# One part of the w_ada sums at double width beside the u projection, three parts beside the chunks and the GLU

## The chip, the cores and the metric

The kernel runs on one core of a Trainium2 chip. The metric is the device time of one launch in microseconds (us). TensorE is called PE here, VectorE DVE, ScalarE ACT, GpSimd POOL, and SyncE, which issues most transfers, SP. Each engine takes its instructions strictly in the order in which they were placed when the kernel was built.

## The reference, cut to what matters

```python
c_act = jax.nn.silu(c)
ada = c_act @ w_ada[l] + b_ada[l]                    # (1, 6*1024)
sh_m, sc_m, g_m, sh_f, sc_f, g_f = jnp.split(ada, 6, axis=-1)
h = modulate(rms_norm(x), sh_m, sc_m)                # h*(1+sc) + sh
proj = h @ w_in[l]                                   # z (1792 columns) and u (512)
y_rwkv = rwkv7_time_mix(z...)                        # a scan over 1024 tokens, 8 heads
y_s5 = s5_mix(u...)                                  # state-space scan, then GELU and a GLU
mix = jnp.concatenate([y_rwkv, y_s5], axis=-1) @ w_out[l]
x = x + g_m[:, None, :] * mix
h = modulate(rms_norm(x), sh_f, sc_f)
x = x + g_f[:, None, :] * ((silu(h @ w_gate) * (h @ w_up)) @ w_down)
return rms_norm(x) * final_gain
```

The six parts of `ada` are numbered 0 to 5 in this order: shift, scale and gate of the mixing half, then shift, scale and gate of the FFN half. Parts 0 and 1 are needed before the first projection, part 2 at the first output of the output projection, parts 3 and 4 for the FFN's input, part 5 at the FFN's output.

## The kernel before, in words

The kernel goes through these stages, with the times of the profiled execution: the start, where x is loaded, normed and transposed (to about 78 us); the u projection (tile `pu`, to 105 us); the z projection with the S5 scan and the preparation of the RWKV chunks (to about 425 us); the chunks of the first half of the tokens, which go on beside the GLU (tile `pglu`, to about 559 us); the output projection of the first half (tile `po`, to 642 us); and the FFN of the first half with the chunks of the second half beside it, and then the rest (to the end).

A part of `ada` is a product of a vector with a 1024 x 1024 block of `w_ada`. `ada_load` (L285) brings columns of the block into tiles `wada`, four transfers of 256 rows each. `ada_acc` (L295 to L300) forms eight products with a scalar per partition and adds them up in `acc`: the first by L295 on DVE, the others by L297 on DVE, or, where `eng` is not DVE, by a multiplication on ACT (L299) and an addition on POOL (L300). `ada_cols` (L306, L307) adds `acc` over the partitions by matmuls with a column of ones into a PSUM tile `pac` and writes `mod`, the table that every modulation and gate reads.

Parts 0 and 1 are summed in the start, 512 columns at a time: two accumulations to a part, with six `wada` tiles in the pool. Parts 2 and 3 go through `ada_steps` (L828), a generator of steps of 256 columns: four accumulations to a part, four `wada` tiles in the pool, which is what one step loads. The argument `mix` decides whose arithmetic a step is: by default every other step (columns 0 and 512 of a part) is on ACT and POOL, the others on DVE. The generator `adg` is woven with the chunks (`c0`) and the GLU (`glg`) at L1254, and its last steps with the second chunks and the finish. Parts 4 and 5 go through a second generator `adl`, all on DVE, which L1434 weaves with the output projection `o0`; L1435 runs what is left of it behind the output projection.

The weave sets the order in which the program is written. A scheduler then places the instructions of each engine by its own estimate of when their inputs are there, so that the order on an engine differs from the written one. The lines of the output projection that matter are: `outproj` loads the parts of y from memory (`yt`, L1295 and L1298), splits them in two (`yhl`, on ACT and POOL), loads and splits the weight (`wraw`, `wo`), multiplies (L1317), and at its end multiplies `po` by `gmb`, the broadcast of part 2 (L1325), and adds x (L1326). `bcast_gate` (L1266, L1267, tile `pgb`) forms `gmb` from `mod`. The finish of a chunk group (`pb`, `pd`, `pv`, `pg`; L949 to L1122) ends in `ld`, which is written to memory as `y_d` and read back as `yt`. The FFN begins with the transposition `ptr` (L1343) of the normed x, and with `pgate` behind it.

Of the kernel before, what the change touches and what calls it, by code (L numbers as in the profile page):

```python
# [29 lines left out]
def kernel(  # L30
# [45 lines left out]
    def pool(name, bufs=1, space=None, side=None, stack=ctx, reuse="tile"):  # L76
        kw = dict(name=name, bufs=bufs)
        if space is not None:
            kw["space"] = space
        if side is not None:  # L80
            kw["side"] = side
        if space != DRAM:
            kw["reuse_waits"] = reuse
        return stack.enter_context(tc.tile_pool(**kw))
# [89 lines left out]
    sp = pool("start", stack=sts, side="right")  # L174
    pst = pool("pstart", stack=sts, space=PSUM)
    pac = pst.tile([P, 512], F32, name="pac")
# [103 lines left out]
    def ada_load(pl, part, j0, n, bufs):  # L280
        c0 = 1024 * part + 128 * j0
        wts = []
        for kk in range(4):
            wt = pl.tile([P, 2, 128 * n], F32, tag="wada", bufs=bufs, name="wada")
            nc.sync.dma_start(wt, w_ada[0, 256 * kk:256 * kk + 256, c0:c0 + 128 * n].rearrange("(k p) n -> p k n", p=P))  # L285
            wts.append(wt)
        return wts

    def ada_acc(pl, wts, n, eng=V):

        acc = pl.tile([P, 128 * n], F32, tag="acc", bufs=2 if n > 2 else 3, name="acc")
        for k in range(8):
            wt = wts[k // 2][:, k % 2, :]
            if k == 0:
                V.tensor_scalar_mul(acc, wt, cact[:, 0:1])  # L295
            elif eng is V:
                V.scalar_tensor_tensor(out=acc, in0=wt, scalar=cact[:, k:k + 1], in1=acc, op0=ALU.mult, op1=ALU.add)  # L297
            else:
                S.mul(wt, wt, cact[:, k:k + 1])  # L299
                G.tensor_tensor(out=acc, in0=acc, in1=wt, op=ALU.add)  # L300
        return acc

    def ada_cols(acc, part, j0, n, ps):

        for j in range(n):
            PE.matmul(ps[:, j:j + 1], lhsT=acc[:, 128 * j:128 * j + 128], rhs=ones[:, 0:1], start=True, stop=True)  # L306
        V.scalar_tensor_tensor(out=mod[:, part, j0:j0 + n], in0=ps, scalar=1.0 if part in (1, 4) else 0.0,  # L307
                               in1=col("b_ada", 8 * part + j0, n), op0=ALU.add, op1=ALU.add)
# [50 lines left out]
    def mods(a0, a1, j0):  # L359
        ada_cols(a0, 0, j0, 4, pac[:, 256 + j0:260 + j0])  # L360
        ada_cols(a1, 1, j0, 4, pac[:, 264 + j0:268 + j0])
# [3 lines left out]
    def u_mm(hf, k, b):  # L365
        for n, (a_, b_) in enumerate(PASS):
            PE.matmul(pu[hf, b], lhsT=uw[b][:, a_, k, :], rhs=hT[hf, k][:, b_, :],  # L367
                      start=(k == 0 and n == 0), stop=(k == 7 and n == 2))
# [169 lines left out]
    wa = [ada_load(sp, part, 0, 4, 6) for part in range(2)]  # L538
# [5 lines left out]
    wa = [ada_load(sp, part, 4, 4, 6) for part in range(2)]  # L544
# [19 lines left out]
    for hf, b in ((0, 2), (0, 3), (1, 2)):  # L564
        for k in range(4):
            u_mm(hf, k, b)
    mods(*acs, 4)
    for hf in range(2):
        for k in range(4, 8):
            modulate(hf, k)  # L570
            for b in range(2):
                u_mm(hf, k, b)
    for hf in range(2):
        for b in range(2):
            u_out(hf, b)
# [250 lines left out]
    def ada_steps(pl, parts, ps, mix=lambda j: j % 4):  # L826

        todo = []  # L828
        def cols():
            acc, part, j = todo.pop(0)  # L830
            ada_cols(acc, part, j, 2, ps("pac2")[:, 0:2])
        for part in parts:
            for j in (0, 2, 4, 6):
                todo.append((ada_acc(pl, ada_load(pl, part, j, 2, 4), 2, V if mix(j) else None), part, j))
                if len(todo) > 2:
                    cols()
                yield
        while todo:
            cols()
            yield  # L840
# [301 lines left out]
    def weave(*gens):  # L1142

        gens = [g if isinstance(g, tuple) else (g, 1) for g in gens]
        while gens:
            for g in list(gens):
                for _ in range(g[1]):
                    if next(g[0], gens) is gens:
                        gens.remove(g)
                        break  # L1150
# [51 lines left out]
    def LIM(g, n):  # L1202
        for _ in range(n):
            if next(g, gens_end) is gens_end:
                return
            yield
# [43 lines left out]
    psx[1] = pool("psp2", stack=sps, space=PSUM)  # L1250
    gls, ads = ExitStack(), ExitStack()
    glg = s5_glu(pool("glp", stack=gls))
    adg = ada_steps(pool("adp2", stack=ads), (2, 3), ps_s)
    weave(c0, (LIM(glg, 18), 2), LIM(adg, 12))  # L1254

    def fd(nm):
# [170 lines left out]
    o0 = outproj(0, xp0, op, ("s", "p", "A", "G"), lambda: pool("gp", stack=gps, side="right"), "a")  # L1427
    weave(seq(c1, finishes(1)), LIM(o0, 4), LIM(late, 4))
    ras.close()
    das = ExitStack()  # L1430
    adl = ada_steps(pool("adp3", stack=das, side="right"), (4, 5), ps_a, lambda j: True)
    weave((LIM(late, 16), 2), o0, (LIM(adl, 2), 1))
    for _ in adl:
        pass  # L1434
    gps.close()  # L1435
    das.close()
    ops.close()
    sps.close()
    now[0] = PARTS[2]
# [54 lines left out]
```

## Time and profile before

| | |
|---|---|
| runs | 1585.34, 1589.63 (median), 1592.18 us |
| the profiled execution's own time | 1592.24 us |
| its span, first to last instruction | 1590.5 us |
| mean granted TensorE clock | 0.937 |
| busy PE, DVE, ACT, POOL | 89%, 60%, 36%, 33% |
| chain that ended last, by engine | PE 62%, DVE 15%, DMA 8%, POOL 7% |
| chain: DVE acc L297, DMA wada | 2% each |

The profiled execution is 2.6 us above the median of the runs and 1.7 us longer than its span. Busy time is counted for each engine; a busy matmul includes what it overlaps with the next, so a group's busy time divided by its count is longer than its pace. "Idle before" with an arrow names what ended an idle time. The granted clock is a share of 2.4 GHz: 1.00 is that level, 0.50 is 1.2 GHz.

### The profile page before, as it was taken

How to read it: one execution, taken by the hardware profiler on the slowest of the kernel's cores; microseconds unless marked ns; L12 is line 12 of the kernel's file. 1: busy time of each engine (PE TensorE's matmuls, PEld its weight loads, DVE VectorE, ACT ScalarE, POOL GpSimd, SP SyncE). 2: the span in 40 equal slices, each digit the busy share in tenths (PEclk: the TensorE clock that was granted, in tenths of full speed). 3: DMA queues.
4: the chain of work that ended last, by engine and by line, in shares of the span. 5: the costliest groups of instructions: out<-in, count | busy, mean ns of one | idle time of the engine just before them, and what ended most of it. 6: DMA issues, size and time to landing. Idle time of an engine off the chain costs nothing.

```text
span 1590.5 us, 22996 instructions
## 1 busy us (share of the span) xinstructions
PE 1421.5 (89%) x9071; PEld 1146.6 (72%) x9071; DVE 948.4 (60%) x1623; ACT 574.5 (36%) x913; POOL 532.4 (33%) x485
## 2 busy tenths in 40 slices
PE   3897898898778878598999999899997999999997
PEld 2775776677667646486777777677786888888885
DVE  6976228889696969854448855445736433333335
ACT  4442345444346453233225422224443222222223
POOL 4369344332154324145000003400251244454543
PEclk8898898998878879799999999899998999999999
DMA  9424754452645355354223224422731423233331
GB/s 292 133 88 138 204 192 144 124 127 75 135 131 148 109 153 187 118 115 100 62 63 117 90 87 99 98 76 66 225 103 38 151 84 107 88 106 93 100 99 54
DMA packets 262060, 187.67 MB, mean 118 GB/s; under 512 B 71606, under 2 KB 233024, under 8 KB 261952
## 3 DMA queue, kind: packets, MB, share of 16 engines
q1 hardware_dynamic: 258224, 178.00, 38.6%
q10 hardware_dynamic: 2912, 7.64, 1.4%
q8 instruction: 71, 1.16, 0.3%
q0 software_dynamic: 816, 0.57, 0.2%
q14 instruction: 37, 0.30, 0.1%
HBM read 157.11 MB, written 31.16 MB: 118 GB/s over the span
## 4 chain that ended last, share of the span: by engine, by line
PE 62%; DVE 15%; DMA 8%; POOL 7%; issue 4%; ACT 3%; SPq 1%; ACTq 0%; DVEq 0%; POOLq 0%
PE pup L270 14%; PE pgate L270 13%; PE pdn L270 13%; PE pz L270 5%; PE po L1317 3%; PE p L1062 3%; DVE acc L297 2%; DMA wada<-in_w_ada_dram 2%; POOL stmp L1006 2%; POOL XU L1008 2%; PE pu L367 2%; PE pY L762 1%; PE pA L962 1%; DMA XU<-x_d 1%; PE pglu L270 1%
## 5 line engine op out<-in xcount | busy, mean ns | idle before, releaser
L270 PE MATMUL pdn<-wd,act 128*128 128x512 f32 x1056 | 268.4, 396 | 0.7 <-DVE x L1366 0.5
L270 PE MATMUL pup<-h,hl_up 128*128 128x512 f32 x1056 | 267.0, 395 | 0.2 <-ACT hl_up L131 0.2
L270 PE MATMUL pgate<-h,hl_g 128*128 128x512 f32 x1056 | 262.8, 395 | 1.2 <-ACT hl_g L131 1.2
L270 PEld LDWEIGHTS pdn<-wd,act 128*128 128x128 f32 x1056 | 196.9, 189 | 46.4 <-issue 2.3
L270 PEld LDWEIGHTS pup<-h,hl_up 128*128 128x128 f32 x1056 | 197.8, 189 | 44.6 <-issue 2.6
L270 PEld LDWEIGHTS pgate<-h,hl_g 128*128 128x128 f32 x1056 | 196.6, 188 | 46.2 <-issue 3.6
L1366 DVE TENSOR_TENSOR x<-pdn,x 128x512 f32<-128x512 f32 x176 | 118.9, 688 | 177.7 <-PE pdn L270 177.0
L270 PE MATMUL pz<-hT,hl_z 128*128 128x256 f32 (+1 forms) x912 | 185.6, 360 | 22.1 <-POOL zm L866 6.7
L270 PEld LDWEIGHTS pz<-hT,hl_z 128*128 128x128 f32 x912 | 150.8, 205 | 52.8 <-ACT zo L872 9.7
L1401 DVE TENSOR_TENSOR rawd<-rawd,gfb 128x1024 f32<-128x1024 f32 x44 | 56.6, 1287 | 106.1 <-DMA rawd<-in_ffn_w_down_dram 83.9
L1317 PE MATMUL po<-wo,yhl 128*128 128x512 f32 x384 | 99.7, 415 | 5.3 <-ACT yhl L1302 2.4
L1317 PEld LDWEIGHTS po<-wo,yhl 128*128 128x128 f32 x384 | 75.1, 200 | 23.7 <-ACT yhl L1302 2.8
L131 ACT CAST hl_up<-raw_up 128x1024 fp32r<-128x1024 f32 x44 | 46.3, 1051 | 123.3 <-PE pup L270 112.0
L131 ACT CAST wd<-rawd 128x1024 fp32r<-128x1024 f32 x44 | 45.8, 1052 | 121.4 <-DVE rawd L1401 91.0
L297 DVE SCALAR_TENSOR_TENSOR acc<-wada,cact,acc 128x256 f32<-128x256 f32 (+1 forms) x112 | 72.1, 653 | 7.5 <-DMA wada<-in_w_ada_dram 6.4
L127 POOL TENSOR_TENSOR yhl<-yt,yhl 128x512 fp32r<-128x512 f32 x16 | 23.4, 1467 | 155.3 <-ACT yhl L1302 149.4
L1006 POOL TENSOR_TENSOR stmp<-LU,XU 128x126 f32<-128x126 f32 (+22 forms) x62 | 31.2, 503 | 127.2 <-DMA LU<-l_d 122.5
L127 POOL TENSOR_TENSOR hl_g<-raw_g,hl_g 128x1024 fp32r<-128x1024 f32 x19 | 45.6, 2397 | 78.9 <-ACT hl_g L131 51.3
L1395 ACT ACTIVATE sgt<-pgate 128x512 f32<-128x512 f32 x44 | 26.4, 600 | 123.5 <-PE pgate L270 123.3
L127 POOL TENSOR_TENSOR wd<-rawd,wd 128x1024 fp32r<-128x1024 f32 x19 | 49.7, 2615 | 57.4 <-ACT wd L131 57.4
L875 POOL TENSOR_TENSOR zo<-zo,zm 128x512 f32<-128x512 f32 x28 | 44.0, 1571 | 72.1 <-ACT zo L872 60.1
L127 POOL TENSOR_TENSOR hl_up<-raw_up,hl_up 128x1024 fp32r<-128x1024 f32 x19 | 49.8, 2620 | 49.5 <-ACT hl_up L131 49.5
(374 smaller groups left out, 2431.3 us busy)
## 6 DMA issues: line engine op xcount, KB each, us to landing
raw_g<-in_ffn_w_gate_dram SPq DMA_DIRECT2D x44, 512.0 KB, 4.0
raw_up<-in_ffn_w_up_dram SPq DMA_DIRECT2D x44, 512.0 KB, 4.0
rawd<-in_ffn_w_down_dram SPq DMA_DIRECT2D x44, 512.0 KB, 3.4
wada<-in_w_ada_dram SPq DMA_DIRECT2D x64, 256.0 KB, 3.1
raw_z<-in_w_in_dram SPq DMA_DIRECT2D x24, 512.0 KB, 5.7
wada<-in_w_ada_dram SPq DMA_DIRECT2D x16, 512.0 KB, 9.6
wraw<-in_w_out_dram SPq DMA_DIRECT2D x32, 256.0 KB, 4.6
zt_d<-zo SPq DMA_DIRECT2D x28, 256.0 KB, 3.0
```

The lines of the kernel that those rows point to most:

```text
L127: (eng or G).tensor_tensor(out=out, in0=a, in1=b, op=ALU.subtract)
L131: S.copy(dst[:, 0], src)
L270: PE.matmul(ps, lhsT=lf(a, k), rhs=rf(b, k), start=(n == 0), stop=(n == 3 * kb - 1))
L297: V.scalar_tensor_tensor(out=acc, in0=wt, scalar=cact[:, k:k + 1], in1=acc, op0=ALU.mult, op1=ALU.add)
L367: PE.matmul(pu[hf, b], lhsT=uw[b][:, a_, k, :], rhs=hT[hf, k][:, b_, :], start=(k == 0 and n == 0), stop=(k == 7 and n == 2))
L875: G.tensor_tensor(out=o, in0=o, in1=zm[:, 0:HT], op=ALU.add)
L1006: SOLVE.tensor_tensor(out=t, in0=LU[:, j, j + 1:32].unsqueeze(2).to_broadcast([P, nt, nk]), in1=X[:, j:j + 1, 0:nk].to_broadcast([P, nt, n ...
L1008: SOLVE.tensor_tensor(out=X[:, j + 1:32, 0:nk], in0=X[:, j + 1:32, 0:nk], in1=t, op=ALU.add)
L1062: PE.matmul(ps[r, h], lhsT=a, rhs=b, start=(n == 0), stop=(n == len(ops) - 1))
L1317: PE.matmul(pss[i], lhsT=yh[k][:, a, 128 * i:128 * i + 128], rhs=wo[:, b], start=(k == 4 and n == 0), stop=(k == 3 and n == 2))
L1366: V.tensor_tensor(out=t, in0=ps, in1=t, op=ALU.add)
L1401: V.tensor_tensor(out=raw, in0=raw, in1=gfb, op=ALU.mult)
```

## The change

Part 2 leaves the steps. Its four transfers for each half of its columns are issued after the first half of the modulations, from the pool of the start with its six tiles, and its two accumulations of 512 columns, all on DVE, are written behind the u projection's matmuls. The steps beside the chunks and the GLU now hold parts 3, 4 and 5: 12 steps of 256 columns instead of 8, every other one on ACT and POOL. The second generator beside the output projection is gone, with its pool.

```diff
@@ -565,11 +565,14 @@
         for k in range(4):
             u_mm(hf, k, b)
     mods(*acs, 4)
+    wa = [(part, j0, ada_load(sp, part, j0, 4, 6)) for part in (2,) for j0 in (0, 4)]
     for hf in range(2):
         for k in range(4, 8):
             modulate(hf, k)
             for b in range(2):
                 u_mm(hf, k, b)
+    for n, (part, j0, w) in enumerate(wa):
+        ada_cols(ada_acc(sp, w, 4), part, j0, 4, pac[:, 272 + 4 * n:276 + 4 * n])
     for hf in range(2):
         for b in range(2):
             u_out(hf, b)
@@ -1250,7 +1253,7 @@
     psx[1] = pool("psp2", stack=sps, space=PSUM)
     gls, ads = ExitStack(), ExitStack()
     glg = s5_glu(pool("glp", stack=gls))
-    adg = ada_steps(pool("adp2", stack=ads), (2, 3), ps_s)
+    adg = ada_steps(pool("adp2", stack=ads), (3, 4, 5), ps_s)
     weave(c0, (LIM(glg, 18), 2), LIM(adg, 12))
 
     def fd(nm):
@@ -1427,13 +1430,8 @@
     o0 = outproj(0, xp0, op, ("s", "p", "A", "G"), lambda: pool("gp", stack=gps, side="right"), "a")
     weave(seq(c1, finishes(1)), LIM(o0, 4), LIM(late, 4))
     ras.close()
-    das = ExitStack()
-    adl = ada_steps(pool("adp3", stack=das, side="right"), (4, 5), ps_a, lambda j: True)
-    weave((LIM(late, 16), 2), o0, (LIM(adl, 2), 1))
-    for _ in adl:
-        pass
+    weave((LIM(late, 16), 2), o0)
     gps.close()
-    das.close()
     ops.close()
     sps.close()
     now[0] = PARTS[2]
```

The placed order shows what this moves. On DVE, beside the u projection, the kernel before has the modulations (`xt`), the lower halves of their splits (`hT`), and then the first split of a z weight (`hl_z`):

```order
L307 SCALAR_TENSOR_TENSOR mod<-pac,cols 128x4 x2
L211 COPY cols<-pac 128x128
L588 TENSOR_SCALAR hbg<-cols 128x4
L589 TENSOR_SCALAR hga<-cols 128x4
L352 TENSOR_SCALAR xt<-xt,mod 128x4x128
L127 TENSOR_TENSOR hT_102<-xt,hT_102 128x512
L352 TENSOR_SCALAR xt<-xt,mod 128x4x128 x3
L127 TENSOR_TENSOR hT_104<-xt,hT_104 128x512
```

The changed kernel has this at the same place, beginning with the first of the two `mod`:

```order
L307 SCALAR_TENSOR_TENSOR mod<-pac,cols 128x4
L295 TENSOR_SCALAR acc<-wada,cact 128x512
L297 SCALAR_TENSOR_TENSOR acc<-wada,cact,acc 128x512
L307 SCALAR_TENSOR_TENSOR mod<-pac,cols 128x4
L295 TENSOR_SCALAR acc<-wada,cact 128x512
L297 SCALAR_TENSOR_TENSOR acc<-wada,cact,acc 128x512 x2
L352 TENSOR_SCALAR xt<-xt,mod 128x4x128
L297 SCALAR_TENSOR_TENSOR acc<-wada,cact,acc 128x512
L352 TENSOR_SCALAR xt<-xt,mod 128x4x128
L297 SCALAR_TENSOR_TENSOR acc<-wada,cact,acc 128x512
L127 TENSOR_TENSOR hT_102<-xt,hT_102 128x512
```

Eleven of the sixteen operations on 512 columns stand between the modulations, the last five behind the last `hT` and ahead of the first `hl_z`.

On PE, the kernel before ends the output projection with these rows, in which four sums of `ada` (`pac`) stand between the last `po` and the next half's `pb`, the gate's `pgb` and the FFN's transpositions:

```order
L1317 MATMUL po<-wo,yhl 128x512 x49
L306 MATMUL pac_5751<-ones,acc 128x1 x2
L1317 MATMUL po<-wo,yhl 128x512 x20
L306 MATMUL pac_5772<-ones,acc 128x1 x2
L306 MATMUL pac_5793<-ones,acc 128x1 x2
L306 MATMUL pac_5797<-ones,acc 128x1 x2
L306 MATMUL pac_5801<-ones,acc 128x1 x2
L949 MATMUL pb<-rz,blk 128x512
L1267 MATMUL pgb<-dgb,ones 128x128 x2
```

The changed kernel has there (line numbers past the first hunk are 3 higher):

```order
L1320 MATMUL po<-wo,yhl 128x512 x14
L924 MATMUL pn<-sq,blk 128x512
L1320 MATMUL po<-wo,yhl 128x512 x62
L952 MATMUL pb<-rz,blk 128x512
L1320 MATMUL po<-wo,yhl 128x512 x20
L965 MATMUL pA<-ar,bk 64x128 x32
L1270 MATMUL pgb<-dgb,ones 128x128 x2
```

No `pac` is left there, `pb` stands among the `po`, and 32 of the next half's `pA` stand ahead of the transpositions.

On SP, behind the last large solve of the chunks, the kernel before issues the transfers for the end of the chunk stage in this order (`y_d` written by the GLU, inputs of the next chunks `kz`, `rz`, `gz`, weights `wraw`):

```order
L285 DMA wada<-in_w_ada_dram 128x2x256 x8
L822 DMA y_d<-zz 128x4x256
L285 DMA wada<-in_w_ada_dram 128x2x256 x2
L790 DMA zz<-z_d 128x4x128 x2
L285 DMA wada<-in_w_ada_dram 128x2x256 x6
L882 DMA kz<-zt_d 128x2x256
L1123 DMA y_d<-ld 128x2x256
```

The changed kernel goes on with `wada` behind these:

```order
L285 DMA wada<-in_w_ada_dram 128x2x256 x9
L885 DMA kz<-zt_d 128x2x256
L1126 DMA y_d<-ld 128x2x256
L885 DMA rz<-zt_d 128x2x256
L885 DMA gz<-zt_d 128x256
L285 DMA wada<-in_w_ada_dram 128x2x256 x2
L825 DMA y_d<-zz 128x4x256
L285 DMA wada<-in_w_ada_dram 128x2x256 x2
L1126 DMA y_d<-ld 128x2x256
L285 DMA wada<-in_w_ada_dram 128x2x256 x7
L885 DMA kz<-zt_d 128x2x256
```

Twelve of the `wada` transfers, three steps' worth, stand behind the first inputs of the next chunks, and the second `kz` behind eleven of them.

## Rows read from the trace of the kernel before

**Rows 1.** Stretches: length, busy (instructions) PE, PEld, DVE, ACT, POOL; clock, DMA, GB/s

```profile
78.00:82.00 4.00, 4.00 (x10) 3.12 (x11) 3.97 (x8) 4.00 (x6) 1.75 (x2) 0.50 0.00 0
82.00:105.00 23.00, 22.89 (x100) 18.38 (x98) 13.35 (x9) 9.76 (x12) 12.51 (x5) 1.00 0.35 115
500.00:559.00 59.00, 46.68 (x637) 38.53 (x635) 53.85 (x122) 29.63 (x59) 19.47 (x20) 0.89 0.42 127
...
574.80:642.00 67.20, 58.00 (x231) 44.11 (x232) 59.18 (x94) 22.76 (x36) 30.69 (x22) 0.91 0.53 164
642.00:661.40 19.40, 6.17 (x23) 4.86 (x23) 16.08 (x45) 4.05 (x10) 0.00 (x0) 0.58 0.49 151
661.40:683.00 21.60, 16.96 (x175) 14.64 (x173) 16.55 (x24) 6.99 (x11) 8.29 (x6) 0.98 0.32 86
683.00:750.00 67.00, 62.31 (x380) 49.95 (x379) 33.14 (x48) 21.18 (x33) 32.89 (x69) 0.96 0.48 108
```

**Rows 2.** Timeline of PE, finish and output projection: start, length, row [idle before]

```profile
558.99 2.07 PE L949 MATMUL pb<-rz,blk 128*128 128x512 f32 x2 [1.00 <-DVE rz L946]
...
574.76 10.17 PE L1317 MATMUL po<-wo,yhl 128*128 128x512 f32 x32 [2.44 <-ACT yhl L1302]
588.24 2.08 PE L1121 MATMUL pg<-gs,g2w 128*128 128x256 f32 x4 [3.30 <-DVE ld L1122]
...
637.27 4.80 PE L1317 MATMUL po<-wo,yhl 128*128 128x512 f32 x20
...
648.25 1.01 PE L306 MATMUL pac<-ones,acc 128*128 128x1 f32 x4 [5.77 <-DVE mod L307]
653.96 0.98 PE L306 MATMUL pac<-ones,acc 128*128 128x1 f32 x4 [4.70 <-DVE acc L297]
657.46 0.98 PE L306 MATMUL pac<-ones,acc 128*128 128x1 f32 x4 [2.51 <-DVE tcol L246]
...
661.41 0.85 PE L1343 MATMUL ptr<-dg,x 128*128 128x128 f32 x3
```

**Rows 3.** Timeline of PE, u projection

```profile
77.94 26.95 PE L367 MATMUL pu<-hT,hl_u 128*128 128x512 f32 x108 [0.37 <-ACT hT L351]
```

**Rows 4.** Timeline of DVE, u projection

```profile
86.60 0.68 DVE L127 TENSOR_TENSOR hT<-xt,hT 128x512 fp32r<-128x512 f32 x1
96.92 1.68 DVE L127 TENSOR_TENSOR hl_z<-raw_z,hl_z 128x1024 fp32r<-128x1024 f32 x1 [9.65 <-PE pu L367]
```

**Rows 5.** Groups by line and shape, 0 to 120 us: busy, mean ns | idle before

```profile
L297 DVE SCALAR_TENSOR_TENSOR acc<-wada,cact,acc 128x512 f32<-128x512 f32 x28 | 24.5, 882 | 1.8 <-DMA wada<-in_w_ada_dram 1.5
```

**Rows 6.** Groups by line and shape, 425 to 530 us

```profile
L300 POOL TENSOR_TENSOR acc<-acc,wada 128x256 f32<-128x256 f32 x28 | 21.7, 777 | 2.2 <-ACT ar L1081 0.6 <-issue 0.3 <-ACT wada L299 0.3
L297 DVE SCALAR_TENSOR_TENSOR acc<-wada,cact,acc 128x256 f32<-128x256 f32 x28 | 16.0, 570 | 1.0 <-DMA wada<-in_w_ada_dram 0.8
```

**Rows 7.** Timeline of DVE, first and last row of five ada steps, and one step

```profile
483.23 0.35 DVE L295 TENSOR_SCALAR acc<-wada,cact 128x256 f32<-128x256 f32 x1
...
494.22 0.34 DVE L295 TENSOR_SCALAR acc<-wada,cact 128x256 f32<-128x256 f32 x1
...
527.34 0.48 DVE L297 SCALAR_TENSOR_TENSOR acc<-wada,cact,acc 128x256 f32<-128x256 f32 x1
```

**Rows 8.** Timeline of SP, chunks and GLU: the issue of eight ada loads

```profile
484.54 16.69 SPq L285 DMA_DIRECT2D wada<-in_w_ada_dram  x8
```

**Rows 9.** Timeline of DVE, one pair of operations at two places

```profile
514.81 3.31 DVE L1114 SCALAR_TENSOR_TENSOR lrs<-ld,cols,lrs 128x256 f32<-128x256 f32 x2
...
531.93 0.87 DVE L1114 SCALAR_TENSOR_TENSOR lrs<-ld,cols,lrs 128x256 f32<-128x256 f32 x2
```

**Rows 10.** Timeline of POOL beside the first of these

```profile
514.19 2.79 POOL L127 TENSOR_TENSOR zhl<-zz,zhl 128x1024 fp32r<-128x1024 f32 x1
```

**Rows 11.** Groups by line and shape, 559 to 661.4 us

```profile
L1325 DVE TENSOR_TENSOR yo<-po,gmb 128x512 f32<-128x512 f32 x8 | 5.5, 685 | 0.0
```

**Rows 12.** Timeline of PE, 740 to 750 us

```profile
746.39 1.92 PE L1028 MATMUL pG<-XU,ak 32*32 32x32 f32 x64 [4.69 <-DMA XU<-x_d]
```

## The prediction

> **What bounds the kernel now.** I read the page's engine shares and its chain first: PE is busy 89% of the span and holds 62% of the chain, so the change can only pay where PE waits. Then I read the busy times by stretch [rows 1]. From 500 to 559 us DVE is the full engine, 53.85 of 59.00 us, and PE has 12.3 us free. From 574.8 to 642 us PE has 58.00 and DVE 59.18 of 67.20 us: neither is full, so they wait for each other. From 642 to 661.4 us PE has only 6.17 of 19.40 us, at a granted clock of 0.58, against 0.91 in the stretch before. That is the hole the change aims at. The timeline of PE says what is in it [rows 2]: three sums of ada columns whose waits, 5.77, 4.70 and 2.51 us, add up to 13.0 us, all for DVE. From 683 us on PE is nearly full again (62.31 of 67.00).
>
> Everything behind 750 us has the same work on every engine, so I price five places: the u projection, the chunk stage, the finish with the output projection, the 22 us behind it, and one wait at 746 us. The sum is made against the profiled execution's own 1592.24 us, which lies 2.6 us over the median of the runs, 1589.63; what comes out is taken off that median.
>
> **1. The u projection.** Sixteen operations on 128x512 come to DVE. At 882 ns [rows 5] they are 14.1 us, taking the two first products as long as the others. In the kernel before, DVE does its last lower half at 86.60 and idles 9.65 us before 96.92 [rows 4]. Eleven new operations stand ahead of that lower half: 11 x 0.882 = 9.7, so it ends at 97.0 instead of 87.3. PE runs 108 matmuls from 77.94 to 104.89 [rows 3], 0.25 us each, and the last six need that lower half: 97.0 + 1.5 = 98.5 still lies before 104.9. The other five operations end at 101.5, the first z weight's lower half (1.68 us) at 103.2, also before. So the work lies beside PE's, and what it costs is that PE meets some lower halves late in the middle of its list, and eight small matmuls. The transfers, 4.2 MB, have room: the DMA share is 0.00 and 0.35 in these stretches [rows 1], though they now stand among the z weights' loads. The bounds: nothing, and +6 if DVE's surplus over its idle time, 14.1 - 9.65 = 4.5, is all paid, with 1.5 for a late transfer. I take +2, nearer to the lower end because the end times fit.
>
> **2. The chunks and the GLU.** Four steps are added, two on DVE, two on ACT and POOL. A DVE step is seven times 0.570 [rows 6] and a first product of 0.35 [rows 7], 4.3 us; of the other kind DVE does only the first product, and POOL 7 x 0.777 = 5.4 us [rows 6]. So DVE gets 2 x 4.3 + 2 x 0.35 = 9.3 us more, POOL 10.9. DVE has 5.2 us free from 500 to 559 [rows 1]. In the placed order the GLU's last norm, some 3 us by an estimate (four operations like L1114's and three as long), leaves this stretch and comes behind the next chunks' `bo`. DVE's list up to there is longer by 9.3 - 3 = 6.3. By the pace of the steps: the five that the kernel before has behind its solve take 527.82 - 483.23 = 44.6 us, 8.9 each [rows 7]. The changed order has nine there: 483.23 + 9 x 8.9 = 563.3, which is 4.3 behind the start of `pb` (558.99). Both readings give +4 to +7; I take +7, since DVE is full here and nothing hides it. The lower bound is 0 (the idle time and the stretch without any ada step from 528 to 559 take it all). The upper bound is the slowest gap between steps, 494.22 - 483.23 = 11.0 [rows 7]: nine of these end at 582.2, +23.
>
> **3. The finish and the output projection.** From `pb` (558.99) to the first transposition (661.41) the kernel before takes 102.4 us [rows 2]. Rebuilt without ada:
> - To the matmuls of the projection. Before, the second pair of `pg` ended at 590.32 after waiting 3.30 us for DVE [rows 2]. Now all `pg` stand before `po`: 590.32 - 558.99 - 3.3 = 28.0 us, as if no `po` went ahead.
> - The 192 `po`. The stretch of 67.20 us has 58.00 us of busy PE [rows 1], of which about 5 are the second `pg` and five sums of ada; 53 are left, and 1 for waits for PSUM banks. At 20 in 4.80 us [rows 2] the `po` alone would be 46.
> - The tail. Four tiles, each a product and an addition of 0.685 us on DVE [rows 11], are 5.5 us; with 3 for the squares and the norm, 8.5. Before, it was 661.41 - 642.07 (637.27 + 4.80) = 19.3 [rows 2], with the 13.0 us of ada waits in it.
>
> 28 + 54 + 8.5 = 90.5, so -12. Bounds: -19 if DVE without its sums of ada lets `po` begin 7 us sooner (before, 32 of them began at 574.76 [rows 2]); -4 if the remaining 160 `po` of before set the pace, (642.07 - 590.32) x 192 / 160 = 62.1 instead of 54. I take the middle, -12.
>
> **4. Behind it.** From 661.4 to 683 PE is idle 4.6 of 21.60 us while DVE has 16.55 [rows 1]. Part of the next chunks' preparation now stands ahead of the transpositions. I take about half, -2.5, between -4.6 and 0.
>
> **5. The wait at 746 us.** PE waits 4.69 us for `XU`, read back from memory [rows 12]. The changed order has 165 matmuls of the FFN before that place instead of 221. The chain that it waits for also starts earlier. Between -4.7 and +5; I take -1.5.
>
> Sum: 2 + 7 - 12 - 2.5 - 1.5 = -7. On the profiled execution 1585.2, on the median **1582.6**, forecast 1583. The forecast's own range is -13 to 0, 1576 to 1590.
>
> **The rivals.**
>
> *A, the chunk stage absorbs the steps.* For it: no step runs from 528 to 559 us, and PE has 12.3 us free there. Against it: DVE is full at 53.85 of 59. Terms 1 and 2 at 0, term 3 at -14: -18, 1572.
>
> *B, the steps set the pace (slower).* The pool has four `wada` tiles, one step's load, and SP issues in order: it spent 16.69 us on eight such transfers because each waits for a tile to come free [rows 8]. In the changed order eleven `wada` issues stand ahead of the second `kz`, and the last sum of ada ahead of `bo`. What queues behind SP's waits is `kz`, `rz`, `wraw` and `yt`, so the preparation and the output projection wait too. At 11.0 us a step term 2 is +23, and the sum 2 + 23 - 12 - 2.5 - 1.5 = +9: 1599. It turns the sign once term 2 passes +14, and counts as slower by 0.5% from +22. Against it: the later steps of before ran at less than 9 us.
>
> *C, DVE and POOL block each other.* A pair of L1114 took 3.31 us at 514.81 [rows 9], while a split of 2.79 us ran on POOL [rows 10], and 0.87 at 531.93 [rows 9]: 2.4 us lost beside one POOL operation. If each of the 14 new POOL additions held DVE up by its own length, 10.9 us, term 2 would be +18 and the sum +4: 1594. Against it: the additions of before ran beside DVE steps of 0.570 mean, not twice as long. The Trainium skill ("SBUF — State Buffer", section "Who interferes with whom") has the rule for it: DVE and GpSimd share a pair of ports as an exclusive lock, so a DVE instruction with two inputs in SBUF is shut out while a GpSimd instruction reads SBUF. The trace agrees with it at 514.81, where L1114 reads two tiles; by that rule moving steps onto POOL is not free for DVE, and its result is this rival's.
>
> *D, the output projection doesn't stream.* If `po` waits for the loads and splits of `yhl` and `wo` rather than for DVE, term 3 is -4 and the sum +1: 1591. For it: the `po` at 574.76 waited 2.44 us for ACT's cast [rows 2]. Against it: POOL has 30.69 of 67.20 us there [rows 1].
>
> **How the numbers follow.** Chances: forecast 0.46, A 0.22, B 0.18, C 0.07, D 0.07. About 0.5%, 7.9 us, is what a measurement of this kernel can tell from no change: faster means under 1581.7, slower over 1597.6. Faster: 0.19 of the forecast, 0.21 of A, 0.40. Slower: 0.13 of B, 0.03 of C, 0.02 of D and 0.02 of the forecast, 0.20. Same: the other 0.40. The range from 1567 to 1602 leaves out the end of A where term 3 is -19 as well, and the part of B beyond +12.
>
> **What would show it.** Term 1: `pu` ends within 6 us of 104.9 and the first `hl_z` doesn't hold `pz`. Term 2: `pb` starts near 568 (2 + 7 behind 558.99); near 559 it is A, from 575 on B, with SP's `wada` issues long and DVE idle for them; in C the L297 and L300 rows are longer than 0.570 and 0.777. Term 3: about 90 us from `pb` to the first `ptr`, no `pac` row behind the last `po`, and a clock well over 0.58 there. In D the waits of `po` name `yhl` or `wo`. The forecast is wrong if the stage grows by over 14 us, or if the hole behind `po` fills with another wait for DVE, the norm's own.

## The result, and the profile after

The changed kernel takes 1576.83 us in the median of 8 runs (1571.9 to 1584.48), the kernel before 1592.12 us in 8 runs (1585.34 to 1599.78). The ratio is 0.9906, with a 95% interval from 0.9884 to 0.9928: 15 us faster. A second measurement, on the chip of three of the variants below, gave 0.9888 (0.985 to 0.9926), 1579.5 against 1594.0 us. The forecast was 7 us faster, 1583 us. The measured time lies at the lower end of the forecast's own range, 1576 to 1590 us; the difference is twice the forecast one and past the 13 us at which that range ended, since the kernel before measured 1592.12 us here and not 1589.63.

The profiled execution took 1576.36 us, its span is 1574.6 us, 15.9 below the span before, at the same mean clock of 0.937. The difference by place, from the start times of rows on PE; "before" is from the groups named, "forecast" is the term of the sum:

| from, to | before | after | difference | forecast |
|---|---|---|---|---|
| start to the end of `pu` [rows 3] | 104.9 | 109.5 | +4.6 | +2 |
| to the first `pG` of the chunk stage | 314.9 | 315.5 | +0.6 | 0 |
| to `pb` [rows 2] | 139.2 | 142.4 | +3.2 | +7 |
| to the first `ptr` [rows 2] | 102.4 | 87.4 | -15.0 | -12 |
| to the first `pgate` [rows 1] | 21.6 | 19.4 | -2.2 | -2.5 |
| to the end | 907.5 | 900.3 | -7.2 | -1.5 |

The first row of `pG` began at 419.76 before and at 425.02 after.

The timeline of PE in the changed kernel, finish and output projection, answers to [rows 2] (start, length, row, idle before):

```profile
567.40 2.07 PE L952 MATMUL pb<-rz,blk 128*128 128x512 f32 x2
...
591.84 2.07 PE L1124 MATMUL pg<-gs,g2w 128*128 128x256 f32 x4 [2.04 <-DVE ld L1125]
...
626.34 15.07 PE L1320 MATMUL po<-wo,yhl 128*128 128x512 f32 x62
641.25 1.05 PE L952 MATMUL pb<-rz,blk 128*128 128x512 f32 x2
641.74 5.10 PE L1320 MATMUL po<-wo,yhl 128*128 128x512 f32 x20
646.77 1.09 PE L965 MATMUL pA<-ar,bk 64*64 64x128 f32 x16
649.11 1.09 PE L965 MATMUL pA<-ar,bk 64*64 64x128 f32 x16 [1.25 <-DVE ak L967]
...
654.83 2.05 PE L1346 MATMUL ptr<-dg,x 128*128 128x128 f32 x16
```

Behind the last `po` there is no sum of ada any more, and PE does 64 `pA` of the next chunks in the 8 us before the transpositions. Before, it waited 13.0 us there for sums of ada, with DVE named as the cause [rows 2]. The stretches of the changed kernel, in the columns of [rows 1]:

```profile
78.00:82.00 4.00, 3.25 (x7) 2.15 (x8) 4.00 (x8) 4.00 (x6) 1.57 (x1) 0.50 0.72 234
82.00:86.00 4.00, 4.00 (x11) 3.15 (x10) 4.00 (x5) 0.86 (x2) 2.27 (x2) 0.50 0.00 2
425.00:567.40 142.40, 113.05 (x1532) 95.09 (x1532) 117.03 (x283) 70.22 (x156) 64.71 (x81) 0.78 0.55 157
596.07:646.84 50.77, 49.37 (x212) 38.73 (x213) 25.75 (x32) 18.65 (x32) 28.50 (x22) 0.97 0.33 100
646.84:654.83 7.99, 4.93 (x68) 3.85 (x68) 7.31 (x19) 4.04 (x10) 0.00 (x0) 1.00 0.06 16
674.27:1574.60 900.33, 867.40 (x4944) 699.78 (x4944) 444.78 (x638) 280.02 (x408) 258.25 (x224) 0.98 0.33 97
```

PE is busy 49.37 of the 50.77 us of `po`, at a clock of 0.97, with DVE at 25.75; before, DVE had 59.18 of 67.20 [rows 1]. The clock behind it is 1.00 instead of 0.58. The last row is to be held against the same view of the kernel before:

```profile
683.00:1590.50 907.50, 873.08 (x4987) 703.92 (x4985) 447.45 (x643) 282.50 (x411) 256.04 (x224) 0.98 0.34 96
```

Behind the first `pgate` PE has 43 instructions and 5.7 us of busy time less; 40 of the 43 are 32 `pA` and 8 `ptm` that now stand ahead of it.

At the start, the timeline of PE shows what the sums cost:

```profile
77.96 2.07 PE L367 MATMUL pu<-hT,hl_u 128*128 128x512 f32 x4 [1.10 <-ACT hT L351]
80.78 17.01 PE L367 MATMUL pu<-hT,hl_u 128*128 128x512 f32 x61 [0.75 <-ACT hT L351]
97.63 0.95 PE L306 MATMUL pac<-ones,acc 128*128 128x1 f32 x8
...
130.59 5.75 PE L270 MATMUL pz<-hT,hl_z 128*128 128x512 f32 x16 [8.06 <-POOL hl_z L127]
```

The 61 matmuls take 17.01 us, 0.279 each against 0.25 before: the clock of 0.50, which ended at 82 us before [rows 1], goes on to 86. The last line belongs to the z projection: the split of a weight on POOL that it waits for came later, and the wait of 5.83 us before is 8.06 us now.

### The profile page after: what moved, and what is told of

The parts are those of the page before. It is cut to its first block, busy times and chain, and to the rows that moved or that the text cites. A ratio compares the mean times of both kernels' runs of the same rounds, so it can differ in the third digit from the quotient of the medians.

```text
span 1574.6 us, 22988 instructions
## 1 busy us (share of the span) xinstructions
PE 1418.4 (90%) x9071; PEld 1145.1 (73%) x9071; DVE 925.9 (59%) x1591; ACT 574.6 (36%) x924; POOL 553.4 (35%) x499
## 4 chain that ended last, share of the span: by engine, by line
PE 58%; DVE 16%; DMA 8%; POOL 8%; ACT 4%; issue 4%; SPq 1%; ACTq 0%; DVEq 0%; POOLq 0%
PE pdn L270 12%; PE pgate L270 12%; PE pup L270 12%; PE pz L270 6%; PE po L1320 3%; PE p L1065 2%; POOL stmp L1009 2%; POOL XU L1011 2%; DVE acc L297 2%; PE pu L367 2%; PE pY L765 1%; DMA wada<-in_w_ada_dram 1%; DMA XU<-x_d 1%; PE pA L965 1%; DMA raw_g<-in_ffn_w_gate_dram 1%
## 5 line engine op out<-in xcount | busy, mean ns | idle before, releaser
L270 PE MATMUL pdn<-wd,act 128*128 128x512 f32 x1056 | 271.8, 398 | 1.0 <-DVE x L1369 0.8
L1320 PE MATMUL po<-wo,yhl 128*128 128x512 f32 x384 | 94.7, 398 | 1.4 <-POOL wo L127 0.8
L127 POOL TENSOR_TENSOR wo<-wraw,wo 128x512 fp32r<-128x512 f32 x32 | 43.0, 1350 | 72.8 <-ACT wo L131 72.8
```

The costliest lines, as they stand in the source:

```text
L127: (eng or G).tensor_tensor(out=out, in0=a, in1=b, op=ALU.subtract)
L270: PE.matmul(ps, lhsT=lf(a, k), rhs=rf(b, k), start=(n == 0), stop=(n == 3 * kb - 1))
L1320: PE.matmul(pss[i], lhsT=yh[k][:, a, 128 * i:128 * i + 128], rhs=wo[:, b], start=(k == 4 and n == 0), stop=(k == 3 and n == 2))
```

## The experiments

Three theories are tested. T, the prediction's: PE waited for DVE's sums in and behind the output projection, and what the sums cost at their new places is a separate, smaller sum. B and C are rivals of the prediction: the four `wada` tiles set the steps' pace, and DVE and POOL block each other. Ratios are to the kernel before on the same chip. In the variants that leave out a part of the sums, its columns of `mod` are set to 1.0, by a line that the diffs here do not show.

### Parts 4 and 5 taken out

The lines that drain the generator and close its pool go with it and are not shown.

```diff
-    adl = ada_steps(pool("adp3", stack=das, side="right"), (4, 5), ps_a, lambda j: True)
-    weave((LIM(late, 16), 2), o0, (LIM(adl, 2), 1))
+    weave((LIM(late, 16), 2), o0)
```

> The kernel before with the second generator taken away: parts 4 and 5 of the sums are left out and their mod columns are set to 1.0. Theory T (the gain is the time in which PE waits for DVE's sums in and behind the output projection; what the sums cost at their new places is separate, about 5 us at the start and 3 us in the chunk stage): pb starts at 559 as before, pb to the first ptr takes 87 us instead of 102, and the whole is 20 to 24 us below the kernel before, 1568 to 1572. Rival O (a good part of the gain comes from the other order that the placement took in the changed kernel, all pg ahead of po, pA ahead of ptr, the FFN's chunks in other gaps, and not from the absence of the sums): pb to ptr stays over 92 us or the whole is less than 14 us below the kernel before, over 1578.

1577.72 us, ratio 0.9909 (0.9881 to 0.9938). `pb` began at 559.32 and the first `ptr` at 644.72, 85.4 us later: T's place and size hold, -17.0 us up to the transpositions. T's total does not: the whole fell by 14 us, not by 20 to 24, and lies at the edge of what rival O had said (less than 14). The first `pgate` was 15.2 us earlier than before (667.8), and the rest to the end took 910.3 us instead of 907.5.

```profile
632.99 2.11 PE L1318 MATMUL po<-wo,yhl 128*128 128x512 f32 x8
635.03 1.08 PE L963 MATMUL pA<-ar,bk 64*64 64x128 f32 x14
636.90 1.09 PE L963 MATMUL pA<-ar,bk 64*64 64x128 f32 x16 [0.78 <-DVE ak L965]
...
644.72 1.95 PE L1344 MATMUL ptr<-dg,x 128*128 128x128 f32 x16
```

This is the same picture as in the changed kernel: with no sums the hole fills with `pA`. The changed kernel does all of the sums and is as fast: it comes to `pb` 8.1 us and to `pgate` 6.5 us later than this one, and needs 900.3 us instead of 910.3 behind it. Why that stretch is shorter is not shown by this run.

### All eight steps woven with the output projection

```diff
-    weave((LIM(late, 16), 2), o0, (LIM(adl, 2), 1))
+    weave((LIM(late, 16), 2), o0, (adl, 1))
```

> The kernel before, but all eight steps of parts 4 and 5 woven with the output projection, instead of two woven and six written behind it. Nothing is moved to another stage. Theory T (DVE is full in the output projection, 59 of 67 us, so the sums cost there whatever their place): the last three sums still stand behind the last po, the 13 us of waits shrink to 6 to 9 and some come into the po: 1585 to 1590. Rival W (only the place where they are written counts; the six written behind are what PE waits for): the waits behind po go to under 3 us and the whole falls to 1577 to 1581, as far as the changed kernel.

1585.06 us, ratio 0.9948 (0.9925 to 0.9972). Three sums still stand behind the last `po`, with 9.3 us of waits, where T had 6 to 9 and a total of 1585 to 1590; rival W is out.

```profile
639.15 0.61 PE L306 MATMUL pac<-ones,acc 128*128 128x1 f32 x4 [0.92 <-DVE mod L307]
645.59 1.01 PE L306 MATMUL pac<-ones,acc 128*128 128x1 f32 x4 [5.83 <-DVE mod L307]
649.12 0.99 PE L306 MATMUL pac<-ones,acc 128*128 128x1 f32 x4 [2.53 <-DVE acc L297]
```

### Parts 4 and 5 half on ACT and POOL

```diff
-    adl = ada_steps(pool("adp3", stack=das, side="right"), (4, 5), ps_a, lambda j: True)
+    adl = ada_steps(pool("adp3", stack=das, side="right"), (4, 5), ps_a)
```

> The kernel before with parts 4 and 5 still beside the output projection, but every other step on ACT and POOL instead of all on DVE. Theory T (PE waits for DVE there, which is at 59 of 67 us): DVE has 16 us less, the waits of the last sums and of po for DVE shrink, pb to the first ptr goes from 102.4 to 92 to 97 us, the whole to 1581 to 1587. Rival Q (it is the sums' chain of load, sum and matmul behind the projection that takes the time, whoever adds): the waits behind the last po stay at 10 us or more, now for POOL, pb to ptr stays over 99 us.

1597.97 us, ratio 1.0023 (0.9996 to 1.005): nothing gained, and T's numbers were wrong. From `pb` to the first `ptr` it took 106.0 us, over 99 as Q had it. The waits behind `po` are 11.4 us on three sums, with POOL named for one of them and DVE for two:

```profile
648.78 0.81 PE L306 MATMUL pac<-ones,acc 128*128 128x1 f32 x4 [3.50 <-DVE mod L307]
654.36 1.01 PE L306 MATMUL pac<-ones,acc 128*128 128x1 f32 x4 [4.78 <-POOL acc L300]
658.49 0.98 PE L306 MATMUL pac<-ones,acc 128*128 128x1 f32 x4 [3.12 <-DVE tcol L246]
```

T has to be worded anew, as Q had it: what PE waits for is the chain of load, sum and matmul of the last steps. Of the chain that ended last from 636 to 662 us, transfers of `wada` hold 35.1% here and DVE's sums (L297) 24.7%; in the kernel before they hold 26.5% and 29.5%. So the waits that are put down to DVE there are in part waits for loads. With all eight steps woven, the loads are gone from that chain (at most 3.0% from 632 to 652 us), and 9.3 us of waits were left: neither the loads nor DVE alone make the hole. Taking additions off DVE was not enough. The pool of these steps has four tiles, too, and whether more of them would have shortened the hole was not run.

### All four parts beside the chunks

The part 2 lines of the change are left out, the second generator is taken away as in the change, and the first gets four parts:

```diff
-    adg = ada_steps(pool("adp2", stack=ads), (2, 3), ps_s)
+    adg = ada_steps(pool("adp2", stack=ads), (2, 3, 4, 5), ps_s)
```

> All of the parts 2 to 5 as 16 steps beside the chunks and the GLU, none at the start, none written beside the output projection. Theory T, with the chunk stage full on DVE: the start is 5 us shorter, the four further steps (9 us of DVE, 11 of POOL) cost 8 to 15 us because five of their sums stand behind pb: 1580 to 1587. Rival S (the stage takes four steps for about 3 us, as it did once): 1573 to 1576. Rival B of the prediction (four wada tiles set the pace at 11 us a step) would show here first: over 1590.

1600.24 us, ratio 1.0058 (1.0037 to 1.0079), 23 us over the changed kernel. By the total that is what B had (over 1590), and T's 1580 to 1587 was wrong. Five sums stand behind `pb`, as T said, but the way from `pb` to the first `po` took 44.8 us instead of 28.7, more than T's price. It is not B's pace: the last eight steps began 6.7 us apart (536.65 to 583.36), with waits of up to 3.88 us for `wada`, not 11 us.

The start of `pb` is a doubtful mark for the end of the chunk stage. Here, and in the kernels without part 2 and with all steps on POOL, it stands ahead of the last matmuls `p` of the chunks; in most of the others behind them. So I also give the stage up to the end of the last `p`: 138.2 us before, 142.4 in the changed kernel, 149.8 here. The first four additional steps cost 4.2 us, the next four 7.4 and, with the sums that stand behind `pb`, 16.1 on the way to `po`. Part 2 beside the u projection is what makes the change pay.

### Eight tiles instead of four

The line is cut short here; all that differs is the last number.

```diff
-                todo.append((ada_acc(pl, ada_load(pl, part, j, 2, 4), 2, ...
+                todo.append((ada_acc(pl, ada_load(pl, part, j, 2, 8), 2, ...
```

> The changed kernel with eight wada tiles instead of four in the pool of the steps. Rival B of the prediction (SP's issues wait for a tile, and this sets the pace of the steps and holds what is queued behind): the stretch from the first pG (425) to pb (567.4) shrinks by 3 us or more, the whole by as much, to 1571 to 1574. Theory T (DVE is full there, the tiles are not the limit): the stretch changes by less than 1.5 us, SP's waits at the wada issues get shorter with no effect, 1575 to 1579.

From the first `pG` (420.64) to `pb` (563.06) it took 142.4 us, as in the changed kernel, and 142.5 to the end of the last `p`: B is out at twelve steps. Yet the whole was 1591.8 us, ratio 0.9997 (0.9969 to 1.0025). In the profiled execution (1584.65 us, the fastest of ten) `pgate` began at 673.2, 1.1 earlier than in the changed kernel, and the rest took 909.7 us instead of 900.3. The edit asks for nothing else there; that the order of the placed instructions is the cause is argued, not shown.

### The steps all on DVE, and all on ACT and POOL

```diff
-    adg = ada_steps(pool("adp2", stack=ads), (3, 4, 5), ps_s)
+    adg = ada_steps(pool("adp2", stack=ads), (3, 4, 5), ps_s, lambda j: True)    # all on DVE
+    adg = ada_steps(pool("adp2", stack=ads), (3, 4, 5), ps_s, lambda j: False)   # all on ACT and POOL
```

> The changed kernel with all twelve steps on DVE, none on ACT and POOL. DVE gets 6 x 7 products of 0.48 to 0.57 us, 20 to 24 us more; POOL 33 us less. Theory T (DVE is what is full): the stretch from the first pG to pb grows from 142.4 us by 10 to 20, the whole to 1585 to 1597. Rival C of the prediction (POOL's additions hold DVE up by their own length, so that a step on POOL costs DVE as much as one of its own): the stretch grows by less than 4 us, the whole under 1581.

> The changed kernel with all twelve steps on ACT and POOL, and only the first product of each on DVE: DVE 20 to 24 us less, POOL 33 us more (65 to 97 us of 142), ACT 21 us more. Theory T: the stretch from the first pG to pb shrinks by 3 to 6 us, to 136 to 139, the whole to 1571 to 1574. Rival C: DVE is held up instead, the L297-like rows and the chunks' own two-input rows on DVE get longer, the stretch stays at 142 or grows, the whole 1577 or more.

All on DVE: 150.0 us from `pG` to `pb`, +7.6, between the two theories, and 1588.16 us, ratio 0.9983 (0.9956 to 1.0011), in T's range. All on POOL: 138.6 us to `pb`, which looks like T's -3.8, but `pb` only stands earlier in the list there:

```profile
562.86 2.07 PE L952 MATMUL pb<-rz,blk 128*128 128x512 f32 x2 [2.16 <-DVE rz L949]
...
566.42 0.42 PE L1065 MATMUL p<-ak,U 64*64 64x64 f32 x4
```

To the end of the last `p` the stage took 142.6 us, as in the changed kernel: T's gain isn't there. The whole was 1591.8 us, ratio 1.0016 (0.9992 to 1.004), with 40.5 us from `pb` to `po`, `pg` waiting 7.56 us for DVE. Both numbers are what rival C had said (142 or more, 1577 or more).

The rows say what became of C. Of each pair the first row is of the changed kernel, the second of the kernel with all steps on POOL (group, busy, mean ns, idle before; 425 to 567 us):

```profile
L300 POOL TENSOR_TENSOR acc<-acc,wada 128x256 f32<-128x256 f32 x42 | 34.1, 812 | 24.2 <-DVE U L1074 11.0 <-PE pn L924 5.5 <-ACT wada L299 5.5
```

```profile
L300 POOL TENSOR_TENSOR acc<-acc,wada 128x256 f32<-128x256 f32 x73 | 59.4, 822 | 28.1 <-PE p L1065 13.6 <-ACT wada L299 5.0 <-DVE acc L295 3.4
```

```profile
L1118 DVE SCALAR_TENSOR_TENSOR lrs<-lrs,cols,bo 128x256 f32<-128x256 f32 x4 | 2.3, 590 | 0.0
```

```profile
L1118 DVE SCALAR_TENSOR_TENSOR lrs<-lrs,cols,bo 128x256 f32<-128x256 f32 x4 | 5.1, 1302 | 0.0
```

POOL's additions keep their length: 777 ns before [rows 6], 812 with half as many again, 822 with 2.6 times as many. DVE's sums beside them do, too: L297 had 570 ns before [rows 6] and has 544 in the changed kernel:

```profile
L297 DVE SCALAR_TENSOR_TENSOR acc<-wada,cact,acc 128x256 f32<-128x256 f32 x42 | 22.8, 544 | 0.2
```

But DVE's other operations on two tensors get longer. Over the groups of one line and shape that both kernels have in the stage, they take 10.8 us more with all steps on POOL, where the additions are 25.3 us more, and 11.3 us less with all steps on DVE, where the 34.1 us of additions are gone; the changed kernel and its repetition differ by 2.3. So C is out at its full price, an addition's own length, but not as a cause: by these two differences, an estimate, an addition costs DVE 0.3 to 0.4 of its length, which is 3 to 5 us for the change's 14 (10.9 us in the prediction).

### Part 2 left out, and part 5 left out

The first drops the part 2 lines of the change, the second makes the steps `(3, 4)`.

> The changed kernel without part 2's loads and sums beside the u projection: part 2 is left out and its mod columns are 1.0. Theory T: pu ends near 105 instead of 109.5, the stretch of clock 0.50 ends at 82 instead of 86, pb comes 5 us earlier, the whole 5 to 7 us below the changed kernel, 1570 to 1572. Rival H (what the start loses is hidden again by later waits for transfers): the whole within 2 us of the changed kernel, 1575 to 1579.

> The changed kernel with parts 3 and 4 alone as steps, eight as in the kernel before; part 5 is left out and its mod columns are 1.0. Theory T (four further steps cost the chunk stage the 3.2 us that it grew): from the first pG to pb 139 us as in the kernel before, instead of 142.4; if everything behind stayed as it was, the whole would be 3 us below the changed kernel. Rival P (each version's order behind the chunk stage is placed anew and comes out some us longer or shorter, whatever was taken away): the stretch shrinks as said, but the whole lies anywhere from 1572 to 1590, with the difference behind pb.

Without part 2 the start behaves as T said: `pu` ends at 105.5, the first `pG` comes at 420.4, `pb` at 562.5, 4.9 us earlier. But `pb` stands ahead of the last `p` there; these end at 566.5, only 1.0 us earlier than in the changed kernel, so most of the saving was gone within the chunk stage. The whole is 1582.52 us, ratio 0.994 (0.992 to 0.9961): less work, and no faster than the changed kernel. From `pb` to the first `ptr` it took 93.4 us (a `pv` waited 6.39 us for ACT), and from `pgate` to the end 907.6. H's sense, that the saving is lost behind, was right; both totals were wrong. Without part 5 the chunk stage took 136.1 us, 6.3 less (7.1 less to the end of the last `p`), and the whole 1576.68 us, ratio 0.9864 (0.9825 to 0.9904), 3 us below the changed kernel on the same chip (1579.52), which the spread of the runs doesn't separate from nothing. That is T's size, but with 136.1 instead of 139 and 906.2 us behind `pgate`, which is what P had said.

### Part 2's sums held back, twice, and the changed kernel again

The sums get a copy of their scalars that depends on the last modulated x, so that they come behind the modulations (the lines that hand `ca` through `ada_acc` are not shown):

```diff
+    held = sp.tile([P, 8], F32, name="held")
+    V.scalar_tensor_tensor(out=held, in0=xts[1][:, 0, 896:904], scalar=0.0, in1=cact, op0=ALU.mult, op1=ALU.add)
     for n, (part, j0, w) in enumerate(wa):
-        ada_cols(ada_acc(sp, w, 4), part, j0, 4, pac[:, 272 + 4 * n:276 + 4 * n])
+        ada_cols(ada_acc(sp, w, 4, ca=held), part, j0, 4, pac[:, 272 + 4 * n:276 + 4 * n])
```

> The changed kernel, with part 2's sixteen operations held back by a dependence: their scalars are a copy of the activated c that is made from the last modulated x, so that they stand behind the last modulation and the last lower half on DVE instead of between them. Theory T on the start (the u projection lost 4.6 us because the sums delayed the lower halves that PE waits for, and PE stayed at clock 0.50 until 86 instead of 82): pu ends at 106 to 107 instead of 109.5, the clock is 1.00 from 82 on, the first pG of the chunk stage starts at 421 to 423 instead of 425.0, the whole 2 to 4 us below the changed kernel. Rival Z (DVE has no room there at all; sums put behind the lower halves delay the S5 constants and the first z weights by as much): pu ends early, but pG starts at 425 or later, the whole within 1 us of the changed kernel or above it.

> The kernel with part 2's sums held back once more: it started the chunk stage 2.6 us earlier than the changed kernel, and yet was at a median of 1595. If the loss is in the fixed order behind the chunk stage (po took 58.6 us instead of 50.8, with pb waiting 4.8 us for DVE in the middle): the median is 10 us or more above the changed kernel on this chip, too, and po again near 58. If it was the chip or the executions: within 5 us of it.

> The changed kernel once more, unaltered, on the same chip as the three that follow. Theory T (its gain is the instructions' places, which are fixed): the median within 4 us of 1576.8, and in the profile pb, the first ptr and pgate within 1 us of 567.4, 654.8 and 674.3. Rival V (the first measurement was of favourable executions, and the variants at 1588 to 1595 show the true level): the median at 1582 or more.

The changed kernel repeated itself: 1579.52 us, with `pb`, `ptr` and `pgate` at 567.8, 656.1 and 675.8, up to 1.6 us from the first places where T had said 1. The held sums took 1595.45 us, ratio 1.0032 (1.0008 to 1.0055), and again 1598.25, ratio 1.0012 (0.9989 to 1.0035). The loss is the kernel's, as the second expectation had it, but only partly at the place that it named (`po` 58.6 and 58.7 us instead of 50.8). The two profiled executions, 1583.5 us (the fastest of twelve, ten of which took 1594.8 or more) and 1598.7 us, differ from each other at the very start, and show how. The first:

```profile
78.10 21.11 PE L368 MATMUL pu<-hT,hl_u 128*128 128x512 f32 x84 [1.10 <-ACT hT L352]
99.05 0.95 PE L307 MATMUL pac<-ones,acc 128*128 128x1 f32 x8
99.86 4.92 PE L368 MATMUL pu<-hT,hl_u 128*128 128x512 f32 x20
```

The second:

```profile
78.52 22.41 PE L368 MATMUL pu<-hT,hl_u 128*128 128x512 f32 x84 [1.10 <-ACT hT L352]
104.99 1.86 PE L307 MATMUL pac<-ones,acc 128*128 128x1 f32 x8 [4.06 <-DVE acc L298]
106.72 7.17 PE L368 MATMUL pu<-hT,hl_u 128*128 128x512 f32 x20
```

Eight tiny matmuls of the sums stand in PE's list ahead of 20 of the projection. In the first execution the sums were ready; in the second DVE's last seven operations took 11.01 us. They waited only 0.17 us for a tile; one of them took 4.83 us instead of 0.74, beside this operation on POOL:

```profile
98.91 4.81 POOL L620 TENSOR_TENSOR s5tw<-pw,ct 128x2304 f32<-128x2304 f32 x1
```

In the first execution it was the other way round: the fourteen sums (L298) took 0.75 us each, and POOL's split of a z weight 7.21 us instead of 2.41. In the second, PE waited 4.06 us for the sums, and its clock fell:

```profile
105.00:110.00 5.00, 5.00 (x16) 4.32 (x17) 1.89 (x3) 0.00 (x0) 0.00 (x0) 0.50 0.34 90
```

The 20 matmuls took 7.17 us instead of 4.92, `pu` ended 9.1 us later, of which 1.7 us were there before the wait, and the first `pG` came at 432.70 instead of 422.44. T on the start was right in the favourable execution (106.6, clock 1.00 from 82, `pG` at 422.4). Yet the version is worse than the changed kernel: in both executions `po` takes 8 us longer, and the sums have no slack left before PE needs them.

## Why the prediction was right, point by point

- **The hole behind the output projection.** Right in place and mechanism. From `pb` to `ptr` 28.7 + 50.8 + 8.0 us against 28 + 54 + 8.5 in the sum. The term was 3 us too small because `po` ran at 0.97 clock with 1.4 us of idle time, better than the 53 us of busy PE of before. Removing the sums alone gave -17.0. Rival D is out by the same rows. What I had read too narrowly is that all of the waits were for DVE: transfers of `wada` hold 26.5% of the chain there.
- **The chunk stage.** +3.2 instead of +7 (+4.2 to the end of the last `p`). Nine steps stand behind the solve, as the order said, from 482.2 to 567.2 us, 9.4 us each. They were to end at 563.3; the stage began 5.3 us later, and they ended 1.4 us earlier than that makes. So the estimate by the steps' pace (+4.3) was near, and the one by DVE's list, which I took, too high. What failed there is "DVE is full here and nothing hides it": from 500 to 559 us DVE has 48.87 of 59 us in the changed kernel, against 53.85 before [rows 1], and over the whole stage it got 4.5 us more (117.03 for 112.53), not 9.3.
- **The start.** +2 was forecast, +4.6 came, +5.3 up to the chunk stage. DVE was done earlier than I had worked out: its last lower half ended at 92.8 us instead of 97.0 and the first z weight's at 102.7 instead of 103.2, since most of the sums took 0.70 to 0.75 us and not 0.882. So the bound of 98.5 for PE held. The term failed on the clock, which stayed at 0.50 for 4 us longer. Ahead of that PE had waited 0.75 us within `pu`, which it did not before [rows 3]; the trace puts this down to ACT's upper halves, not to the lower halves on DVE that I had named. That the wait kept the clock down is likely but not shown: with held sums it was at 1.00 from 82 us in one execution and still at 0.50 until 84 in the other, with no such wait in either. The term failed on the next stage as well: POOL's split of a z weight took 5.81 us instead of 2.34, beside an S5 operation on DVE with two inputs that had begun before it. The Trainium skill ("SBUF — State Buffer", section "Who interferes with whom") says that such a pair excludes each other; the trace agrees here, and in the two executions with held sums, where once POOL's operation and once DVE's was the one that took longer.

```profile
123.58 4.87 DVE L619 TENSOR_TENSOR s5w<-pwr,bb 128x2048 f32<-128x2048 f32 x1
```

```profile
124.72 5.81 POOL L127 TENSOR_TENSOR hl_z<-raw_z,hl_z 128x1024 fp32r<-128x1024 f32 x1
```

- **Behind the transpositions.** The term up to `pgate` was right (-2.2 for -2.5). The step on the wait at 746 us failed: it stayed, 4.59 us for 4.69 [rows 12], 26 us earlier; the chain that it waits for moved as far as the matmuls in front of it.

```profile
720.53 1.92 PE L1031 MATMUL pG<-XU,ak 32*32 32x32 f32 x64 [4.59 <-DMA XU<-x_d]
```

  What failed most is that the sum priced nothing else behind `pgate`: PE has 43 instructions less there. Of the -7.2, 1.5 us are less idle time of PE and 5.7 less busy time. About 3 of these are the 40 matmuls that went ahead, an estimate by the lengths of their rows; the rest goes with less time at half clock (the granted clock's loss summed over stretches of 10 us is 18.7 us before and 17.1 after, or 10.4 and 7.5 if each stretch counts by PE's busy time).
- **The size of the whole.** -15.9 lies near rival A's -18, but not for A's reason: the stage did not absorb the steps, and the start cost more. Up to `pgate` the sum was -5.5 and -8.7 came, so the mechanism carries the forecast that far. The other -7.2, for a forecast of -1.5, has a cause that I had not named and is in part luck, by the next point.
- **What stays open.** From `pgate` to the end the versions took between 896 and 910 us in their profiled executions with nearly the same work: 907.5 before, 900.3 and 902.6 after, 910.3, 907.6, 906.2, 909.7, 908.9 in the kernels without parts 4 and 5, without part 2, without part 5, with eight tiles and with all steps woven. All of that spread lies in the FFN of the first half and the second chunks beside it: from the last `po` of the second half to the end, every profiled execution took 390 to 392 us. PE's idle time behind `pgate` makes up about half of it (32.9 us after, 38.0 without parts 4 and 5). Each edit has the instructions placed anew. No run held that order fixed, so how much of the 15 us is the removed wait and how much a fortunate order behind it isn't settled; by the place where it is gained, 8.7 us are in front of `pgate`. Of the variants, only those without part 5, with parts 4 and 5 half on ACT and POOL, and with held sums the second time ran on a chip together with the changed kernel's repetition; the others are held against it by way of the kernel before.

## What to carry to other kernels

A small sum that ends in a tiny matmul costs little while it is early (4.6 us at the start here) and stops a whole in-order matmul list when it is late (13.0 us of waits): give it a stage in which its last result is ready long before PE's list comes to it. Look for such holes by the waits behind the last matmul of a stage, and expect later work to move into a hole that is closed, so that part of the gain shows up elsewhere. A variant that is ahead by 7 us at `pgate` can lose most of it behind (without part 5: 667.1 for 674.3, and 906.2 us behind it for 900.3); read each stage by itself, and repeat the best. End a stage at a mark that means the same in every version: a row that was placed earlier looks like a gain.

## What the runs showed of the hardware

- Behind a wait of 4.06 us on PE in the u projection the clock was 0.50 from 105 to 110 us, and 20 matmuls took 7.17 us instead of 4.92.
- The same program lost time on either side of the pair DVE and POOL: with held sums, a DVE sum of 128x512 took 4.83 us instead of 0.74 beside a POOL operation of 4.81 us in one execution, and a POOL split 7.21 us instead of 2.41 beside DVE's sums in the other.
- Executions of one kernel on one core differ by more than the medians of many variants do: the kernel with held sums took 1583.5 to 1604.1 us in one measurement, the changed one 1571.9 to 1584.5, with the lower mean granted clock in the longer ones (0.940 at 1571.9, 0.934 at 1584.5).
